# Attention: queries and keys converted in two slots each, both copies of a head's sum ahead of its difference, compressed values split once

## The chip, the cores and the metric

One core of a Trainium2 chip runs the whole kernel. The time is that of one execution on the device in microseconds (us); three executions of the kernel before took 1440.02 to 1446.53 us, with a median of 1442.75 us. Engines are named as in the profile: PE multiplies matrices, DVE (VectorE) and ACT (ScalarE) work elementwise, POOL (GpSimd) does elementwise work and some transfers, SP only issues transfers.

## What is computed

One block of a decoder on 512 tokens of width 2048: a normalised input is projected; a part of it goes through an attention with three branches, another through sliding means, both are merged with gates, projected and added to the input; then a mixture of experts follows. The change concerns the attention. Cut to that:

```python
q, k_slc, k_swa = [_partial_rope(_rms(a, gain), cos, sin) for ...]   # 16 heads, 4 key groups
kc, vc = _compress(k_cmp), _compress(v_cmp)                          # 31 blocks
p_cmp = _masked_softmax(q @ kc * scale, cmp_end <= t); o_cmp = p_cmp @ vc
p     = _masked_softmax(q @ ks * scale, ...);          o_slc = p @ vs
p     = _masked_softmax(q @ kw * scale, ...);          o_swa = p @ vw
o = g0 * o_cmp + g1 * o_slc + g2 * o_swa
attn_branch = einsum("bshd,hde->bshe", o, w_head_out)
```

All is float32. With 512 tokens both the selected and the sliding branch see all earlier tokens.

## The kernel before, in words

Float32 products are made of pairs. A number is stored as a rounded copy and the difference to it; ACT makes the copy, DVE or POOL the difference, and PE multiplies copy by copy, copy by difference and difference by copy, adding up in PSUM (`mm3`, lines 134 to 136; `evac_split`, lines 139 and 140). So almost every product needs an ACT step, then a DVE or POOL step, then PE.

The program is one long list per engine, in the order in which the Python code emits it. `run` (line 201) walks over the pieces of the large projections (`qkv`, `u` for the pooling input, `wp`, `z` for the merge gates, `wo`), and after every part of a piece it makes one `step`: it emits the first function of the list `deferred`, if there is one, and then the functions of the next slot of `side`. The slots of the attention come from a table of numbers, `PLAN` (line 41), by `attention_slots` (line 835). Per group of four heads (four groups, g = 0 to 3) there are in slots relative to the group's start `w0`: the queries `at_q` at -6, the keys `at_k` at -4, the compressed branch `at_c0` to `at_c4` at -4, -2, -1, 1 and 3; and then each head, 8 or 9 slots apart, with four score steps `at_qk`, four scalings `at_scale`, six transposing steps `at_T` (slots 9 to 14), six products `at_pv` (11 to 16) and `at_out` at 18. So the queries and keys of one group lie among the last transposes of the group before.

Names used below. `qn` is the normalised query and key tile; `qT` its transposed queries in PSUM, `q` the pair made of them (partitions 0 to 63 the copy, 64 to 127 the difference); `kT` and `k` (`k1`, `k2`) the same for keys; `kw` the compressed keys. `s` are scores in PSUM, `m` their maxima and sums, `p` the exponentials, `pt` their transpose in PSUM, `pth` and `ptl` the pair made of that, `o` the sum over positions of a head, `oh` and `ol` its pair, `vcg` the compressed values of a group, one block per head, masked by `hmask`. `pl` and `ph` are the pair of the pooling. `qT`, `kT`, `scT` and `s` share one PSUM tile (tag S), and all `pt` share another (tag tr), each with a single buffer: the next transposes wait until both halves of the pair are read out.

After a group's projection, the queries and keys are normalised by steps in `deferred`, one per slot: squares of the first half, squares of the second half, inverse root (12 small instructions), norm, gains, rope. The steps of the pooling share this list.

A head's sum `o` is stored as `oh` (a copy, ACT), `ol` partitions 64 to 127 (the difference, DVE) and `ol` partitions 0 to 63 (a second copy, ACT), in this order (lines 818 to 820); one tile holds both parts of `ol`.

Of the kernel before, what the change touches and what calls it, by code (L numbers as in the profile page):

```python
# [11 lines left out]
F32 = mybir.dt.float32  # L12
# [10 lines left out]
NT = 4  # L23
# [28 lines left out]
    'c0': -4,  # L52
# [24 lines left out]
def hybrid_block_kernel(  # L77
# [37 lines left out]
    def s_tile(name):  # L115
        return psum.tile([128, 2, 512], F32, tag="S", name=name)
# [168 lines left out]
    vcr = mix.tile([128, NKV, 64], F32, name="vcr")  # L285
# [35 lines left out]
    gain = mix.tile([128, 6, 64], F32, name="gain")  # L321
# [18 lines left out]
    def late_loads():  # L340
        q = nc.sync
        for i in range(4):
            q.dma_start(gain[:, i], q_norm_g.to_broadcast([128, 64]))
        q.dma_start(gain[:, 4], k_norm_slc_g.to_broadcast([128, 64]))
        q.dma_start(gain[:, 5], k_norm_swa_g.to_broadcast([128, 64]))
# [187 lines left out]
    def cmp_value():  # L533
# [5 lines left out]
        V.tensor_copy(vcr, po[:, 0:256].rearrange("p (g d) -> p g d", g=4))  # L539
# [50 lines left out]
    def qkv(g):  # L590
# [6 lines left out]
        def done(ps):  # L597
# [13 lines left out]
            q3 = qn.rearrange("p t h d -> p t (h d)")  # L611
# [16 lines left out]
            def gains():  # L628
                V.tensor_tensor(q3, q3, gain.rearrange("p h d -> p (h d)")[:, None, :].to_broadcast([128, NT, 384]),
                                op=OP.mult)  # L630

            def rope():
# [11 lines left out]
            deferred.extend([lambda: squares(0), lambda: squares(1), inverse, norm, gains, rope,  # L644
                             lambda: marks.add(f"qkv{g}")])
# [7 lines left out]
    def at_q(g):  # L653
        att, qn = pools["att"], QN[g]
        st = s_tile(f"qT{g}")
# [4 lines left out]
        for h in range(4):  # L660
            QT[4 * g + h] = att.tile([128, S], F32R, tag="q", name=f"q{g}_{h}", bufs=4)
            A.copy(QT[4 * g + h][0:64], st[64 * (h % 2):64 * (h % 2) + 64, h // 2])
        for h in range(4):
# [3 lines left out]
    def at_k(g):  # L667
# [4 lines left out]
        st = s_tile(f"kT{g}")  # L672
        for t in range(NT):
            T.transpose(st[:, 0, t * 128:(t + 1) * 128], qn[:, t, 4:6].rearrange("p h d -> p (h d)"), ident)
        ur = [(u, slice(64 * r, 64 * r + 64)) for u in range(2) for r in range(2)]
# [62 lines left out]
    def at_c4(g):  # L738
# [3 lines left out]
        for t in range(NT):  # L742
# [5 lines left out]
        vcf = att.tile([128, 4, 64], F32, tag="sm", name=f"vcf{g}")  # L748
        vcg = att.tile([128, 4, 128], F32R, tag="vcg", name=f"vcg{g}")
        V.tensor_tensor(vcf, vcr[:, g, None, :].to_broadcast([128, 4, 64]),  # L750
                        hmask[:, :, None].to_broadcast([128, 4, 64]), op=OP.mult)
        A.copy(vcg[:, :, 0:64], vcf)
        V.tensor_sub(vcg[:, :, 64:128], vcf, f(vcg[:, :, 0:64]))
        pools["vcg", g] = vcg
# [45 lines left out]
    def at_pv(head, i):  # L800
# [13 lines left out]
        if i == 5:  # L814
# [3 lines left out]
            A.copy(oh, o)  # L818
            V.tensor_tensor(ol[64:128], o[0:64], f(oh[0:64]), op=OP.subtract)
            A.copy(ol[0:64], o[0:64])  # L820
# [14 lines left out]
    def attention_slots():  # L835
# [6 lines left out]
        for g in range(NKV):  # L842
# [10 lines left out]
            at(w0 + PLAN['q'], at_q, g)  # L853
            at(w0 + PLAN['k'], at_k, g)
# [742 lines left out]
```

## Time and profile before

| what | value |
|---|---|
| three executions, median | 1442.75 us |
| profiled execution, its time | 1442.58 us |
| profiled execution, its span | 1440.8 us |
| mean granted PE clock | 0.984 |
| PE busy | 1388.4 us, 96% of the span |
| DVE busy | 825.1 us, 57% |
| ACT busy | 765.6 us, 53% |
| POOL busy | 445.4 us, 31% |

The attention runs from about 140 to 800 us, beside the projections. A row of the order of time gives the start in us from the start of the span, the duration, the engine, the line of the kernel, the operation, what it writes and reads, its form and how many were merged; in brackets stands how long the engine had been idle, and what released it. PE is the matrix multiplication, PEld the loading of its weights, which runs beside it.

### The profile page before, as it was taken

The page shows a single profiled execution, that of the slowest core. Times are in us where ns is not written, and L with a number is a line of the kernel's source. Part 1 is how long each engine was busy: PE and PEld are TensorE (multiplying, and loading weights), DVE is VectorE, ACT ScalarE, POOL GpSimd, SP SyncE. Part 2 cuts the span into 40 slices and gives each one's busy share as a digit, 9 for nine tenths or more (in the row PEclk, how much of TensorE's full clock was granted, in tenths as well). Part 3 has the DMA queues.
Part 4 walks back from the last instruction along what each step waited for, and adds up shares of the span by engine and source line. Part 5 has one row for each costly group of instructions (what it writes and reads, how often), then busy time and mean ns, then how long its engine had stood idle before and what let it go on. Part 6 is the DMA issues. An engine that isn't in the chain of part 4 may idle for free.

```text
span 1440.8 us, 18395 instructions
## 1 busy us (share of the span) xinstructions
PE 1388.4 (96%) x6638; PEld 1138.2 (79%) x6638; DVE 825.1 (57%) x1258; ACT 765.6 (53%) x1289; POOL 445.4 (31%) x289
## 2 busy tenths in 40 slices
PE   8998999989999999999999999999999999999995
PEld 7877788778778788788888888888887777777774
DVE  4663773666463453555543202453255899999995
ACT  4543356564666465655665322332242687777784
POOL 0044342322333343243434455211021322222221
PEclk9999999999999999999999999999999999999998
DMA  6344233233333333343434453785675899999994
GB/s 224 94 115 123 80 102 87 77 107 85 91 116 111 92 93 87 96 117 97 109 110 125 117 141 108 224 326 166 226 252 175 279 362 367 367 358 354 330 363 84
DMA packets 193188, 249.88 MB, mean 173 GB/s; under 512 B 50384, under 2 KB 137536, under 8 KB 191264
## 3 DMA queue, kind: packets, MB, share of 16 engines
q1 hardware_dynamic: 176640, 199.13, 43.6%
q0 software_dynamic: 11808, 41.09, 10.0%
q10 hardware_dynamic: 4640, 8.40, 1.6%
q8 instruction: 54, 0.88, 0.3%
q14 instruction: 46, 0.38, 0.1%
HBM read 225.49 MB, written 35.65 MB: 181 GB/s over the span
## 4 chain that ended last, share of the span: by engine, by line
PE 79%; DVE 10%; ACT 6%; issue 2%; DMA 1%; POOL 1%; ACTq 0%; SPq 0%; POOLq 0%; DVEq 0%
PE z L134 7%; PE z L136 7%; PE z L135 7%; PE gu L136 4%; PE gu L134 4%; PE gu L135 4%; PE wo L134 4%; PE wo L136 4%; PE wo L135 4%; PE qkv L135 2%; PE qkv L134 2%; PE qkv L136 2%; PE dn L134 2%; PE dn L135 2%; PE dn L136 2%; PE xT L1245 2%
## 5 line engine op out<-in xcount | busy, mean ns | idle before, releaser
L197 POOL TENSOR_TENSOR lo_z<-raw_z,hi_z 128x1024 fp32r<-128x1024 f32 x64 | 153.4, 2401 | 200.5 <-ACT hi_z L196 192.8
L134 PE MATMUL z<-hT,hi_z 128*128 128x512 f32 x512 | 204.1, 399 | 0.0
L136 PE MATMUL z<-hT,lo_z 128*128 128x512 f32 x512 | 200.7, 392 | 0.0
L135 PE MATMUL z<-hT,hi_z 128*128 128x512 f32 x512 | 200.2, 391 | 0.0
L140 DVE TENSOR_TENSOR ptl<-pt,pth 128x512 fp32r<-128x512 f32 (+1 forms) x96 | 57.8, 602 | 177.0 <-ACT pth L139 176.8
L197 DVE TENSOR_TENSOR lo_gu<-raw_gu,hi_gu 128x2048 fp32r<-128x2048 f32 x64 | 146.8, 2294 | 9.8 <-ACT hi_gu L196 4.2
L196 ACT CAST hi_gu<-raw_gu 128x2048 fp32r<-128x2048 f32 x64 | 122.3, 1911 | 18.7 <-PE gu L136 9.9
L778 ACT ACTIVATE p<-s,m 128x128 f32<-128x128 f32 (+3 forms) x128 | 66.4, 523 | 115.6 <-DVE m L776 112.4
L197 POOL TENSOR_TENSOR lo_qkv<-raw_qkv,hi_qkv 128x1024 fp32r<-128x1024 f32 x28 | 70.6, 2521 | 173.8 <-ACT hi_qkv L196 148.6
L136 PEld LDWEIGHTS z<-hT,lo_z 128*128 128x128 f32 x512 | 96.5, 189 | 21.2
L135 PEld LDWEIGHTS z<-hT,hi_z 128*128 128x128 f32 x512 | 96.7, 189 | 18.6
L134 PEld LDWEIGHTS z<-hT,hi_z 128*128 128x128 f32 x512 | 96.9, 189 | 18.3
L134 PE MATMUL gu<-hi_gu,xh 128*112 128x512 f32 x256 | 106.4, 416 | 0.1
L134 PE MATMUL qkv<-hi_qkv,hT 128*128 128x512 f32 x256 | 103.5, 404 | 0.1
L135 PE MATMUL qkv<-lo_qkv,hT 128*128 128x512 f32 x256 | 101.4, 396 | 0.3 <-POOL lo_qkv L197 0.3
L136 PE MATMUL gu<-hi_gu,xl 128*112 128x512 f32 x256 | 101.7, 397 | 0.0
L136 PE MATMUL qkv<-hi_qkv,hT 128*128 128x512 f32 x256 | 101.5, 396 | 0.0
L134 PE MATMUL wo<-hi_wo,y 128*128 128x512 f32 x256 | 101.1, 395 | 0.0
L135 PE MATMUL gu<-lo_gu,xh 128*112 128x512 f32 x256 | 100.4, 392 | 0.0
L136 PE MATMUL wo<-hi_wo,y 128*128 128x512 f32 x256 | 99.8, 390 | 0.0
L135 PE MATMUL wo<-lo_wo,y 128*128 128x512 f32 x256 | 99.7, 389 | 0.0
L1313 POOL DMA_INDIRECT out_dram<-y,idx x18 | 60.1, 3337 | 107.7 <-ACT hi_gu L196 88.6
(419 smaller groups left out, 3193.7 us busy)
## 6 DMA issues: line engine op xcount, KB each, us to landing
raw_z<-in_w_in_dram SPq DMA_DIRECT2D x128, 256.0 KB
raw_gu<-in_w_expert_gate_dram SPq DMA_DIRECT2D x59, 512.0 KB
raw_gu<-in_w_expert_up_dram SPq DMA_DIRECT2D x59, 512.0 KB
raw_dn<-in_w_expert_down_dram SPq DMA_DIRECT2D x28, 1024.0 KB
raw_wo<-in_w_out_dram SPq DMA_DIRECT2D x32, 512.0 KB
raw_qkv<-in_w_in_dram SPq DMA_DIRECT2D x32, 256.0 KB
raw_qkv<-in_w_in_dram SPq DMA_DIRECT2D x128, 64.0 KB
raw_u<-in_w_in_dram SPq DMA_DIRECT2D x16, 512.0 KB
```

The source lines that it names most:

```text
L134: T.matmul(ps, ah, bh, start=start, stop=False)
L135: T.matmul(ps, ah, bl, start=False, stop=False)
L136: T.matmul(ps, al, bh, start=False, stop=stop)
L140: V.tensor_tensor(lo, src, f(hi), op=OP.subtract)
L196: A.copy(self.hi[sl], self.raw[sl])
L197: self.eng.tensor_sub(self.lo[sl], self.raw[sl], f(self.hi[sl]))
L778: A.activation(p[:, b], v[:, b], AF.Exp, bias=m[:, b:b + 1], scale=0.125, accum_out=m[:, 2 + b:3 + b])
L1245: T.transpose(pt[:, j * RS:(j + 1) * RS], self.xr[:, k0 * 128 + j:(k0 + 4) * 128:4], ident[0:RS, 0:RS])
L1313: ins = G.indirect_dma_start(out=dst, out_offset=bass.IndirectOffsetOnAxis(ap=idx, axis=0), in_=src, in_offset=None, bounds_check=n - 1, o ...
```

## The change

Six edits, which leave PE's rows as they were and in their order:

1. Queries: `at_q` makes the transposes of all four heads and the pairs of two; the pairs of the other two come a slot later (`at_q_half`).
2. Keys: the same in `at_k` and `at_k_half`; `at_c0` comes a slot later, at -3.
3. Head's sum: both ACT copies first, then DVE's difference.
4. Compressed values: they are split into a pair once for all groups (`vhl`, in place of `vcr`), and each group's `vcg` is made by four ACT scalings with `hmask`, in place of a product and a difference on DVE and a copy on ACT.
5. Normalisation: empty steps between the squares, behind them and ahead of the rope, in groups 1 to 3; the gains are held three times in place of six and applied in two instructions (three loads fewer).
6. Pooling: the copy `ph` and the difference `pl` are two steps in place of one.

```diff
-    'c0': -4,
+    'c0': -3,
...
-        V.tensor_copy(vcr, po[:, 0:256].rearrange("p (g d) -> p g d", g=4))
+        pv = po[:, 0:256].rearrange("p (g d) -> p g d", g=4)
+        A.copy(vhl[:, :, 0:64], pv)
+        V.tensor_tensor(vhl[:, :, 64:128], pv, f(vhl[:, :, 0:64]), op=OP.subtract)
...
-                V.tensor_tensor(q3, q3, gain.rearrange("p h d -> p (h d)")[:, None, :].to_broadcast([128, NT, 384]),
+                V.tensor_tensor(qn[:, :, 0:4], qn[:, :, 0:4], gain[:, 0, None, None, :].to_broadcast([128, NT, 4, 64]),
+                                op=OP.mult)
+                V.tensor_tensor(qn[:, :, 4:6], qn[:, :, 4:6], gain[:, None, 1:3].to_broadcast([128, NT, 2, 64]),
                                 op=OP.mult)
...
-            deferred.extend([lambda: squares(0), lambda: squares(1), inverse, norm, gains, rope,
-                             lambda: marks.add(f"qkv{g}")])
+            ready, pause = (lambda: marks.add(f"qkv{g}")), [lambda: None] * (g > 0)
+            deferred.extend([lambda: squares(0), *pause, lambda: squares(1), *pause, inverse, norm, gains, *pause, rope,
+                             ready])
...
-        st = s_tile(f"qT{g}")
+        st = pools["qT"] = s_tile(f"qT{g}")
...
-        for h in range(4):
+        at_q_half(g, 0)
+
+    def at_q_half(g, p):
+        att, st = pools["att"], pools["qT"]
+        for h in (2 * p, 2 * p + 1):
             QT[4 * g + h] = att.tile([128, S], F32R, tag="q", name=f"q{g}_{h}", bufs=4)
             A.copy(QT[4 * g + h][0:64], st[64 * (h % 2):64 * (h % 2) + 64, h // 2])
-        for h in range(4):
+        for h in (2 * p, 2 * p + 1):
...
-        vcf = att.tile([128, 4, 64], F32, tag="sm", name=f"vcf{g}")
-        vcg = att.tile([128, 4, 128], F32R, tag="vcg", name=f"vcg{g}")
-        V.tensor_tensor(vcf, vcr[:, g, None, :].to_broadcast([128, 4, 64]),
-                        hmask[:, :, None].to_broadcast([128, 4, 64]), op=OP.mult)
-        A.copy(vcg[:, :, 0:64], vcf)
-        V.tensor_sub(vcg[:, :, 64:128], vcf, f(vcg[:, :, 0:64]))
-        pools["vcg", g] = vcg
+        vcg = pools["vcg", g] = att.tile([128, 4, 128], F32R, tag="vcg", name=f"vcg{g}")
+        for h in range(4):
+            A.mul(vcg[:, h], f(vhl[:, g]), hmask[:, h:h + 1])
...
             A.copy(oh, o)
+            A.copy(ol[0:64], o[0:64])
             V.tensor_tensor(ol[64:128], o[0:64], f(oh[0:64]), op=OP.subtract)
-            A.copy(ol[0:64], o[0:64])
...
+            at(w0 + PLAN['q'] + 1, at_q_half, g, 1)
             at(w0 + PLAN['k'], at_k, g)
+            at(w0 + PLAN['k'] + 1, at_k_half, g, 1)
...
-            deferred.extend([lambda st=1 << i: double(st) for i in range(g + 1)] + [mean, halves])
+            deferred.extend([lambda st=1 << i: double(st) for i in range(g + 1)] + [mean, half, rest])
```

Where the rows move, at three places. The lines in the rows of the change are those of the changed kernel.

First, the queries of group 1. On ACT before, from the copies of the queries on:

```order
L662 CAST q_0_2716<-qT_2707 64x512
L662 CAST q_1_2718<-qT_2707 64x512
L662 CAST q_2_2720<-qT_2707 64x512
L662 CAST q_3_2722<-qT_2707 64x512
L899 CAST ph_2597<-s_4_2666 128x1024
L830 COPY a_2745<-a_2742 128x512
L831 DMA adram<-a_2745 128x512
L139 CAST pth<-pt_0_2748 128x512
L196 CAST hi_wp_2757<-raw_wp_2755 128x1024
L139 CAST pth<-pt_1_2773 128x512
L677 CAST k_1_2780<-kT_2782 64x512 x4
L699 CAST kw_1244<-kcT 128x32
```

On ACT in the change, from the same copies:

```order
L668 CAST q_0_2716<-qT_2707 64x512
L668 CAST q_1_2718<-qT_2707 64x512
L907 CAST ph_2597<-s_4_2666 128x1024
L836 COPY a_2738<-a_2735 128x512
L837 DMA adram<-a_2738 128x512
L139 CAST pth<-pt_0_2741 128x512
L668 CAST q_2_2748<-qT_2707 64x512
L668 CAST q_3_2750<-qT_2707 64x512
L196 CAST hi_wp_2756<-raw_wp_2754 128x1024
L139 CAST pth<-pt_1_2773 128x512
L687 CAST k_1_2780<-kT_2782 64x512 x2
L139 CAST pth<-pt_2_2808 128x256
```

Two query copies and two key copies now stand behind the next `pth`. On DVE before, from the query differences on:

```order
L665 TENSOR_TENSOR q_0_2716<-qT_2707,q_0_2716 64x512
L665 TENSOR_TENSOR q_1_2718<-qT_2707,q_1_2718 64x512
L665 TENSOR_TENSOR q_2_2720<-qT_2707,q_2_2720 64x512
L665 TENSOR_TENSOR q_3_2722<-qT_2707,q_3_2722 64x512
L900 TENSOR_TENSOR pl_2598<-s_4_2666,ph_2597 128x1024
L140 TENSOR_TENSOR ptl<-pt_0_2748,pth 128x512
L140 TENSOR_TENSOR ptl<-pt_1_2773,pth 128x512
L679 TENSOR_TENSOR k_1_2781<-kT_2782,k_1_2780 64x512 x4
```

On DVE in the change, from the same differences:

```order
L671 TENSOR_TENSOR q_0_2716<-qT_2707,q_0_2716 64x512
L671 TENSOR_TENSOR q_1_2718<-qT_2707,q_1_2718 64x512
L140 TENSOR_TENSOR ptl<-pt_0_2741,pth 128x512
L671 TENSOR_TENSOR q_2_2748<-qT_2707,q_2_2748 64x512
L671 TENSOR_TENSOR q_3_2750<-qT_2707,q_3_2750 64x512
L910 TENSOR_TENSOR pl_2598<-s_4_2666,ph_2597 128x1024
L140 TENSOR_TENSOR ptl<-pt_1_2773,pth 128x512
L689 TENSOR_TENSOR k_1_2781<-kT_2782,k_1_2780 64x512 x2
L140 TENSOR_TENSOR ptl<-pt_2_2808,pth 128x256
L689 TENSOR_TENSOR k_1_2781<-kT_2782,k_1_2780 64x512 x2
```

The first `ptl` moved from behind four differences and `pl` to behind two, and the second pair stands ahead of the second `ptl`.

Second, DVE in the compressed branch of group 1 (`pcl` is the difference of its probabilities). Before:

```order
L140 TENSOR_TENSOR pcl_3079<-pc_3073,pch_3078 128x512
L750 TENSOR_TENSOR vcf_3082<-vcr,hmask 128x256
L753 TENSOR_TENSOR vcg_3083<-vcf_3082,vcg_3083 128x4x64
L783 RECIPROCAL m_1_3042<-m_1_3042 128x2
L900 TENSOR_TENSOR pl_2872<-s_8_3023,ph_2871 128x1024
L772 TENSOR_TENSOR s_2_3115<-s_2_3115,causal 128x2x128
L775 TENSOR_REDUCE m_2_3122<-s_2_3115 128x2
L776 TENSOR_SCALAR m_2_3122<-m_2_3122 128x2
```

In the change:

```order
L140 TENSOR_TENSOR pcl_3079<-pc_3073,pch_3078 128x512
L789 RECIPROCAL m_1_3042<-m_1_3042 128x2
L778 TENSOR_TENSOR s_2_3114<-s_2_3114,causal 128x2x128
L781 TENSOR_REDUCE m_2_3121<-s_2_3114 128x2
L782 TENSOR_SCALAR m_2_3121<-m_2_3121 128x2
L910 TENSOR_TENSOR pl_2872<-s_8_3023,ph_2871 128x1024
```

`vcf` and `vcg` are gone, and `pl` stands behind the next maximum.

Third, DVE in group 2's normalisation, beside the first head of the group's heads that are still running (`sq` and `ss` are the squares and their sums, `pool` a product of the pooling). Before, from the second squares to the inverse's first row:

```order
L920 TENSOR_SCALAR pool_1_3503<-pm_1_3496,cols 128x512
L618 TENSOR_TENSOR sq_1_3506<-qn_3459 128x768
L619 TENSOR_REDUCE ss_3461<-sq_1_3506 128x12
L819 TENSOR_TENSOR ol_3516<-o_3317,oh_3515 64x512
L783 RECIPROCAL m_3_3423<-m_3_3423 128x2
L772 TENSOR_TENSOR s_0_3525<-s_0_3525,causal 128x256
L775 TENSOR_REDUCE m_0_3530<-s_0_3525 128x2
L776 TENSOR_SCALAR m_0_3530<-m_0_3530 128x2
L920 TENSOR_SCALAR pool_3_3552<-pm_3_3545,cols 128x512
L622 TENSOR_SCALAR ss_3461<-ss_3461 128x24
```

In the change, from the head's difference `ol`:

```order
L826 TENSOR_TENSOR ol_3513<-o_3317,oh_3512 64x512
L789 RECIPROCAL m_3_3423<-m_3_3423 128x2
L778 TENSOR_TENSOR s_0_3522<-s_0_3522,causal 128x256
L781 TENSOR_REDUCE m_0_3527<-s_0_3522 128x2
L782 TENSOR_SCALAR m_0_3527<-m_0_3527 128x2
L930 TENSOR_SCALAR pool_3_3549<-pm_3_3542,cols 128x512
L617 TENSOR_TENSOR sq_1_3552<-qn_3459 128x768
L618 TENSOR_REDUCE ss_3461<-sq_1_3552 128x12
L140 TENSOR_TENSOR ptl<-pt_0_3555,pth 128x512
L789 RECIPROCAL m_0_3527<-m_0_3527 128x2
L140 TENSOR_TENSOR ptl<-pt_1_3594,pth 128x512
```

The second squares moved from ahead of `ol` to behind the head's maximum, and the inverse, whose twelve rows stood ahead of the head's first `ptl`, now begins four rows below the last one shown, ahead of the third `ptl`.

## Rows read from the trace of the kernel before

**Rows 1.** The page, part 2: PE's busy tenths in 40 equal slices.
```profile
PE   8998999989999999999999999999999999999995
```

**Rows 2.** A stretch: us, busy us of each engine (instructions), PEclk, DMA share, GB/s.
```profile
100.00:800.00 700.00, 671.97 (x3239) 558.59 (x3238) 357.85 (x682) 385.35 (x870) 252.10 (x122) 0.99 0.37 101
```

**Rows 3.** Order of time, group 1: start, us, instruction, count, [idle before <- releaser].
```profile
319.60 2.80 DVE L665 TENSOR_TENSOR q<-qT,q 64x512 fp32r<-64x512 f32 x4 [4.03 <-ACT q L662]
...
321.52 0.59 ACT L139 CAST pth<-pt 128x512 fp32r<-128x512 f32 x1 [0.40 <-ACT a L830]
...
324.43 1.11 PE L797 MATMUL pt<-ident,p 128*128 128x128 f32 x4 [3.96 <-DVE ptl L140]
...
325.34 1.06 PE L674 MATMUL kT<-ident,qn 128*128 128x128 f32 x4
```

**Rows 4.** Order of time, the same place in group 2.
```profile
484.08 0.59 ACT L139 CAST pth<-pt 128x512 fp32r<-128x512 f32 x1 [0.40 <-ACT a L830]
...
485.73 1.12 PE L797 MATMUL pt<-ident,p 128*128 128x128 f32 x4 [3.34 <-DVE ptl L140]
...
486.64 1.06 PE L674 MATMUL kT<-ident,qn 128*128 128x128 f32 x4
```

**Rows 5.** Order of time, groups 1 and 2, from c4 to the scores.
```profile
361.83 0.41 ACT L752 CAST vcg<-vcf 128x256 fp32r<-128x256 f32 x1 [2.31 <-DVE vcf L750]
...
369.19 0.50 PE L769 MATMUL s<-k,q 128*128 128x512 f32 x1 [2.57 <-ACT p L778]
...
526.35 0.50 PE L769 MATMUL s<-k,q 128*128 128x512 f32 x1 [0.58 <-ACT p L778]
```

**Rows 6.** Order of time, group 2's first head with the norm steps.
```profile
412.01 0.58 ACT L820 CAST ol<-o 64x512 fp32r<-64x512 f32 x1 [2.18 <-DVE ol L819]
...
413.63 0.33 PE L797 MATMUL pt<-ident,p 128*128 128x128 f32 x1 [2.15 <-ACT p L787]
...
413.74 0.17 DVE L622 TENSOR_SCALAR ss<-ss 128x24 f32<-128x24 f32 x1
...
416.13 0.18 DVE L131 SCALAR_TENSOR_TENSOR ss<-rtmp,ss 128x24 f32<-128x24 f32 x1
...
423.13 1.75 DVE L629 TENSOR_TENSOR qn<-qn,gain 128x1536 f32<-128x1536 f32 x1
...
425.27 0.42 PEld L797 LDWEIGHTS pt<-ident,p 128*128 128x128 f32 x4 [0.21 <-DVE ptl L140]
```

**Rows 7.** Stretches behind three gaps, columns as in rows 2.
```profile
163.60:167.00 3.40, 3.40 (x11) 2.62 (x10) 0.81 (x2) 3.18 (x5) 0.00 (x0) 0.50 0.02 5
324.00:327.50 3.50, 3.07 (x12) 2.79 (x13) 1.07 (x2) 1.64 (x3) 1.86 (x1) 0.51 0.11 18
484.50:491.30 6.80, 5.57 (x17) 4.75 (x18) 3.00 (x5) 4.23 (x8) 1.00 (x1) 0.50 0.40 117
```

**Rows 8.** Groups by form: count, busy us, mean ns | idle before, releaser.
```profile
L819 DVE TENSOR_TENSOR ol<-o,oh 64x512 fp32r<-64x512 f32 x16 | 10.9, 684 | 24.8 <-ACT oh L818 24.6
...
L787 ACT ACTIVATE p<-p,m 128x128 f32<-128x128 f32 x32 | 10.9, 387 | 0.0
...
L820 ACT CAST ol<-o 64x512 fp32r<-64x512 f32 x16 | 9.3, 581 | 17.2 <-DVE ol L819 17.2
```

**Rows 9.** Order of time, group 0: the query and key chain, then a head.
```profile
162.65 1.09 PE L658 MATMUL qT<-ident,qn 128*128 128x128 f32 x8 [2.28 <-DVE qn L642]
...
177.42 0.50 PE L709 MATMUL scT<-q,kw 128*128 128x512 f32 x1 [0.33 <-DVE kw L700]
...
177.47 1.22 DVE L895 SCALAR_TENSOR_TENSOR s<-s,u 128x1024 f32<-128x1024 f32 x1
...
220.54 0.66 PE L797 MATMUL pt<-ident,p 128*128 128x128 f32 x4 [0.58 <-DVE ptl L140]
```

**Rows 10.** Order of time, group 0: POOL's difference beside DVE's gains.
```profile
155.92 3.20 POOL L197 TENSOR_TENSOR lo_u<-raw_u,hi_u 128x1024 fp32r<-128x1024 f32 x1 [3.04 <-ACT hi_u L196]
...
156.91 3.83 DVE L629 TENSOR_TENSOR qn<-qn,gain 128x1536 f32<-128x1536 f32 x1
```

More of the change, by code (lines that the diff above doesn't have):

```diff
@@ L284, in hybrid_block_kernel @@
     gates = mix.tile([128, NT, 48], F32, name="gates")
-    vcr = mix.tile([128, NKV, 64], F32, name="vcr")
+    vhl = mix.tile([128, NKV, 128], F32R, name="vhl")
     kcT = mix.tile([128, 128], F32, name="kcT")
@@ L320, in hybrid_block_kernel @@
     sc = mix.tile([128, 5, 2, 8], F32, name="sincos")
-    gain = mix.tile([128, 6, 64], F32, name="gain")
+    gain = mix.tile([128, 3, 64], F32, name="gain")
     posi = early.tile([128, 5], I32, name="posi")
@@ L341, in late_loads @@
         q = nc.sync
[L342 to L345, printed above, removed]
+        for i, g_ in enumerate((q_norm_g, k_norm_slc_g, k_norm_swa_g)):
+            q.dma_start(gain[:, i], g_.to_broadcast([128, 64]))
         q.dma_start(gainc, k_norm_cmp_g.to_broadcast([128, 64]))
@@ L610, in done @@
             q2 = qn.rearrange("p t h d -> p (t h) d")
-            q3 = qn.rearrange("p t h d -> p t (h d)")
             rs = ss[:, 1].rearrange("p t h -> p (t h)")
@@ L671, in at_k, with at_k_half @@
         KK[g] = (k1, k2)
-        st = s_tile(f"kT{g}")
+        st = pools["kT"] = s_tile(f"kT{g}")
         for t in range(NT):
             T.transpose(st[:, 0, t * 128:(t + 1) * 128], qn[:, t, 4:6].rearrange("p h d -> p (h d)"), ident)
-        ur = [(u, slice(64 * r, 64 * r + 64)) for u in range(2) for r in range(2)]
+        at_k_half(g, 0)
+    def at_k_half(g, u):
+        (k1, k2), st = KK[g], pools["kT"]
+        ur = [(u, slice(64 * r, 64 * r + 64)) for r in range(2)]
         for u, rr in ur:
@@ L896, in mean, with half, rest @@
                 V.tensor_tensor(s[:, :, 0:w - 1], e[:, :, 0:w - 1], u[:, :, 0:w - 1], op=OP.subtract)
-            def halves():
+            def half():
                 A.copy(ph, cur[0])
+            def rest():
                 V.tensor_sub(pl, cur[0], f(ph))
```

## The prediction

> **What bounds the kernel now.** I read the page first, then the stretches, then TensorE's (PE's) idle time with its releasers, last the order of time around each gap. PE's row of slices is at nine tenths or more from the attention's end almost to the last slice [rows 1]. A stage with PE full cannot get shorter here, since PE's own instructions and their order are the same before and after. What can be won lies where PE stands idle: in the stretch from 100 to 800 us, which holds the whole attention, PE is busy 671.97 of 700 us [rows 2]. So 28 us is the ceiling, less what belongs to the end of the projection. These idle spells are single gaps, and each has a cause in VectorE (DVE) or ScalarE (ACT) queues a few us earlier. The largest are: 3.96 us in group 1 and 3.34 us in group 2, where the transposes `pt` wait for the difference `ptl` behind the query work [rows 3, 4]; 2.57 us in group 1, where the scores `s` wait for an exponential [rows 5]; 2.15 us in group 2, where `pt` waits for a scaled `p` [rows 6]. After the gaps of rows 3 and 4 the granted clock is 0.51 for 3.5 us and 0.50 for 6.8 us, the lower of its two levels, 1.2 GHz [rows 7].
>
> **The change, part by part.**
>
> *Compressed values (c4).* DVE loses `vcf` and the `vcg` difference in each group, and ACT loses one copy and its wait for `vcf`, 2.31 us in group 1 [rows 5]. ACT gains four scalings of 128x128; the same form takes 387 ns [rows 8], so 4 x 0.39 = 1.5 us at most, less than the 2.31 us wait they replace plus the copy of 0.41. Behind them on ACT are the reciprocal's product, the scaled `p` and the next exponentials. In group 1 the pooling difference `pl` also moves behind the next maximum on DVE. Since ACT and DVE both lose over 2 us ahead of the exponential on which PE waited 2.57 us, I count that gap as gone, and likewise the 0.58 us of group 2 [rows 5]: **-3.15**. Should ACT's four be twice as dear, 1.5 us more would still leave half of the gap closed. The one-time split of `vhl` runs before the first attention work, with DVE idle behind it: 0.
>
> *Queries in two slots.* Before, DVE stands idle for 4.03 us until ACT has made its copies, four differences then take 2.80 us from 319.60, and `ptl` stands behind them and `pl` [rows 3]. Now ACT makes two copies of 0.58 [rows 8], 1.2 us less ahead of `pth`, and DVE two differences, and then `ptl`. In group 1 the head's sum comes earlier too, with its two ACT copies side by side, so DVE's difference and what follows it start up to 0.58 later; so `pth` moves from 321.52 to about 320.9, `ptl` ends at 322.2 and `pt` starts at 322.3 in place of 324.43. But the key transposes `kT` come next on PE, and `kT` takes the PSUM tile of `qT`; it must wait for the second pair: two more ACT copies behind `pth` (2 x 0.58, to 322.7) and two differences (1.4, to 324.1). `kT` then starts at 324.15 in place of 325.34: **-1.2**. In group 2 nothing delays DVE: `pth` at 484.08 - 1.18 = 482.9, `pt` at 484.25, the second pair done at 486.1, `kT` at 486.1 in place of 486.64 [rows 4]: **-0.5**. So one long gap becomes two, the second behind the second pair. Groups 0 and 3 had no such gap.
>
> *The clock behind these gaps.* At half rate 3.5 and 6.8 us cost 1.7 and 3.4 us [rows 7]. The gaps left, about 1.8 + 1.25 us in each group, are 0.2 to 0.9 us shorter in sum than before; the 2.57 us of rows 5 was followed by no stretch at the low level, the 2.28 us gap ahead of `qT` in group 0 was, at half rate in the trace just behind it [rows 7, 9]. Bounds 0 and 5.1; I take one stretch of the three: **-1.7**.
>
> *Heads' sums.* ACT's second copy no longer waits for DVE's difference (17.2 us over 16 heads [rows 8]), but the difference now waits for that copy. Where DVE came late, as in group 2 behind the squares, this helps: ACT stood idle for 2.18 us until 412.01, so oh was done at 409.8; ACT's copy now ends at 410.4 and the difference at 411.1 in place of 412.0, and the scaling of `p` stands behind the difference and not behind ACT's copy, another 0.3 less: `p` is ready about 1.15 us sooner, and the gap of 2.15 shrinks to 1.0 [rows 6]. That is given back: the twelve small steps of the inverse (413.74 to 416.3, 2.6 us) move from in front of the head's first `ptl` to in front of its third, where the gains (1.75) stood; the weight load behind that `ptl` already waits 0.21 [rows 6], so PE waits 2.6 - 1.75 = 0.9 more. Together **-0.25**. Where DVE was waiting for oh, 24.8 us idle in all [rows 8], the scaling of `p` now starts after ACT's copy, the difference and the reciprocal (0.58 + 0.68 + 0.2 behind oh) in place of the difference and the copy (0.68 + 0.58), 0.2 later. Between no cost, where PE comes later than `p`, and 16 x 0.2 = 3.2 I take **+0.9**, nearer the low end, because only some heads have `pt` at the heels of `p`.
>
> *`pl` a step later.* In group 0 `ptl` is no longer behind `pl`, and the 0.58 us gap there goes [rows 9]: **-0.55**.
>
> *Keys in two slots, `c0` a slot later.* The second pair of key differences and `kw` come behind a step of other work. In group 0 this is the pooling's mean, 1.22 us and two small steps; `scT` already waits 0.33 for `kw` [rows 9]. I take 0.8 there and 0.2 in each later group, between 0 and 1.5 each: **+1.4**.
>
> *Gains in two instructions, norm steps further apart.* The same 1536 elements with one start more: **+0.1** in group 0, where `qT` waits for this chain. The pauses fill slots of later heads; the rope still ends well ahead of `qT`. Three loads fewer on SP's queue: they land long before use, 0.
>
> Here one row speaks of more. The gains of group 0 took 3.83 us where those of group 2 took 1.75, while POOL's `lo_u` ran from 155.92 for 3.20 us [rows 6, 10]. So DVE work that lands beside a POOL difference can lose some 2.1 us. The Trainium skill, "SBUF — State Buffer", section "Who interferes with whom", says that a DVE instruction with two SBUF inputs and a GpSimd instruction that reads SBUF exclude each other for a whole instruction, and that ACT waits for neither; the rows agree. By it the move of `vcg` to ACT is safe, and each moved norm step is a new ticket: one loss of 2.1 us in front of a waiting `pt` would take the sum to 1439.6.
>
> The sum: -3.15 - 1.2 - 0.5 - 1.7 - 0.25 - 0.55 + 0.9 + 1.4 + 0.1 = -4.95. The profiled execution took 1442.58 us, 0.2 below the median of the three runs (1442.75), so I forecast **1437.5 us**, -0.35%. The runs shown spread from 1440.02 to 1446.53, so about 0.5% (7.2 us) is what can be told from no change; my forecast lies inside that.
>
> **The rivals.**
>
> *Faster: the clock stays up and the small costs hide.* If the shorter pairs of gaps leave the clock at its upper level in both groups (3.4 more) and PE never meets `p` or `kw` late (2.3 more), it comes to 1431.8. For it: the gap of 2.57 us without a drop. Against it: both pairs still sum to about 3 us with some 0.6 us of work between, and the 2.28 us gap was followed by a drop.
>
> *Slower: the norm steps in front of `ptl`.* Squares, inverse, norm, gains and rope of groups 1 to 3 now stand in more slots, each in front of some `ptl` or `ol`. Where DVE is the late engine, PE pays the difference. If in each of the three groups the inverse costs 0.9 as in group 2, one step loses 2.1 to POOL, and the query and clock gains fail as well (3.4 us), it comes to 1437.5 + 2 x 0.9 + 3 x 2.1 + 3.4 = 1449, +0.45%; it ends above today's time once these steps cost over 1.7 us in each group. Against it: DVE has only 358 busy us of 700 here [rows 2], and outside the places named the `ptl` wait for ACT, not for DVE.
>
> *The halves do not do what they say.* If DVE's first pair still starts only when ACT is through with all four, or `kT` waits so long for the second pair that nothing is won, the query terms and the clock go (3.4): 1440.9. For it: before, the first difference did wait for all four copies although it needs one.
>
> **How the numbers follow.** My forecast, with its terms within about 3 us, 0.57; the halves without effect 0.11; faster 0.25; slower 0.07. Of the forecast, some 0.02 lies beyond 0.5% faster. So faster 0.27, same 0.66, slower 0.07. The range from 1431.5 to 1443.5 takes the clock term's far end with most of the fast case, and no gain at all on the other side; it leaves out the slow case and the lower half of the fast one.
>
> **What would show it.** The profile after should show: no `vcf`, four ACT scalings per group without a wait, and no gap at `s` at the places of rows 5; two DVE query differences starting after ACT's second copy, a gap at `pt` of about 1.8 us in groups 1 and 2 and a new one of about 1.2 at `kT`; a gap of about 0.9 at the fourth `pt` of the head behind the inverse in group 2; ACT's second copy of a head's sum without idle time, and DVE's difference 0.6 later. PE should stay full after 800 us. It is wrong if the sum of PE's gaps from 100 to 800 falls by much more or less than 3 us besides the clock, if new gaps at `pt` or `o` exceed those removed, or if the low clock after `qT` lasts as long as before.

## The result and the profile after

The changed kernel is slower: a median of 1453.52 us in five runs (1450.47 to 1455.84), against 1445.04 us for five runs of the kernel before (1440.02 to 1446.53); the ratio is 1.0074, 95% interval 1.006 to 1.0088. The forecast was 1437.5 us. The profiled execution has a span of 1454.1 us, 13.3 more than before. It is the slowest of the five, 2.3 us above their median, and at 0.980 its mean granted clock is the lowest (0.982 to 0.985 in the others), so its span overstates the change. These are the page's first line, PE's line of its part 1 and PE's row of slices, after the change.

```profile
span 1454.1 us, 18414 instructions
...
PE 1396.6 (96%) x6638; PEld 1142.7 (79%) x6638; DVE 826.1 (57%) x1254; ACT 768.4 (53%) x1302; POOL 443.0 (30%) x289
...
PE   9998899989999999989999999999999999999996
```

PE has the same 6638 instructions, so I put its 8.2 us more of busy time (1388.4 before) down to the clock; the other 5.1 us are idle time. Stretches of the changed kernel show where (us, busy us of PE, PEld, DVE, ACT and POOL with counts, PEclk, DMA share, GB/s); the first holds what [rows 2] held, work that now lasts some 12 us longer.

```profile
100.00:812.00 712.00, 677.29 (x3237) 560.71 (x3236) 358.53 (x677) 388.24 (x883) 251.34 (x122) 0.98 0.36 99
```
```profile
327.70:331.10 3.40, 3.40 (x10) 2.68 (x9) 3.37 (x3) 1.16 (x2) 1.42 (x1) 0.50 0.21 52
488.20:495.00 6.80, 6.08 (x17) 4.93 (x18) 2.72 (x4) 2.43 (x4) 2.37 (x1) 0.50 0.30 77
641.80:645.20 3.40, 3.40 (x11) 2.63 (x10) 0.65 (x1) 3.00 (x6) 0.00 (x0) 0.51 0.61 196
665.60:669.00 3.40, 3.40 (x10) 2.63 (x9) 0.00 (x0) 0.59 (x1) 0.00 (x0) 0.50 0.61 154
1116.20:1126.40 10.20, 9.53 (x31) 7.87 (x31) 5.77 (x36) 1.01 (x3) 0.00 (x0) 0.50 0.73 245
1133.30:1136.70 3.40, 3.22 (x12) 2.62 (x13) 1.25 (x2) 1.06 (x2) 1.34 (x2) 0.51 0.19 58
```

In the attention PE now idles 712 - 677.29 = 34.7 us in place of 28.0. The stretches at 1.2 GHz behind the old places of [rows 7] are as long as before, there are two new ones at 641.8 and 665.6, and at the start of the experts there are 13.6 us at half rate in two stretches, where before there was this one.

```profile
1105.80:1112.50 6.70, 6.70 (x20) 5.64 (x21) 4.32 (x27) 0.21 (x1) 0.00 (x0) 0.50 0.83 304
```

So 6.7 us of the loss are idle time in the attention, and the longer time at half rate costs 6.8 us more: 3.4 in the attention and 3.4 at the experts. The second half of that need not belong to the change: over 1100 to 1140 us PE's granted clock is 0.91 before and 0.83 here, and 0.91 again in the two runs further down that take one difference off POOL and keep the rest of the change.

Now the places that the prediction named, in the order of time after the change (start us, us, instruction, count, [idle before <- releaser]).

```profile
322.15 1.39 DVE L671 TENSOR_TENSOR q<-qT,q 64x512 fp32r<-64x512 f32 x2 [2.84 <-ACT q L668]
...
325.44 0.33 PE L803 MATMUL pt<-ident,p 128*128 128x128 f32 x1 [1.85 <-DVE ptl L140]
...
327.21 0.33 PE L680 MATMUL kT<-ident,qn 128*128 128x128 f32 x1 [1.11 <-DVE q L671]
...
364.41 1.29 ACT L760 ACTIVATE vcg<-vhl,hmask 128x128 fp32r<-128x128 f32 x4
...
371.09 0.39 PE L775 MATMUL s<-k,q 128*128 128x512 f32 x1
...
414.18 0.33 PE L803 MATMUL pt<-ident,p 128*128 128x128 f32 x1 [0.91 <-ACT p L793]
...
427.68 0.33 PE L803 MATMUL pt<-ident,p 128*128 128x128 f32 x1 [0.88 <-DVE ptl L140]
...
487.15 0.33 PE L803 MATMUL pt<-ident,p 128*128 128x128 f32 x1 [1.85 <-DVE ptl L140]
488.92 0.48 PE L680 MATMUL kT<-ident,qn 128*128 128x128 f32 x1 [1.11 <-DVE q L671]
```

The long gap of [rows 3, 4] has become two, 1.85 at `pt` and 1.11 at `kT`, in groups 1 and 2; the scores of [rows 5] wait for nothing; the 2.15 of [rows 6] is 0.91, with a new 0.88 behind the inverse. All these numbers were forecast. The loss stands at places where no gap was:

```profile
317.00 2.24 DVE L904 TENSOR_TENSOR s<-pe,u 128x14 f32<-128x14 f32 x1
...
315.81 3.40 POOL L197 TENSOR_TENSOR lo_u<-raw_u,hi_u 128x1024 fp32r<-128x1024 f32 x1 [3.54 <-ACT hi_u L196]
...
320.50 0.33 PE L803 MATMUL pt<-ident,p 128*128 128x128 f32 x1 [1.67 <-ACT p L793]
...
336.44 2.20 DVE L710 TENSOR_TENSOR kw<-kcT,kw 128x32 fp32r<-128x32 f32 x1
...
336.25 2.35 POOL L197 TENSOR_TENSOR lo_qkv<-raw_qkv,hi_qkv 128x1024 fp32r<-128x1024 f32 x1 [7.12 <-ACT hi_qkv L196]
...
338.70 0.51 PE L719 MATMUL scT<-q,kw 128*128 128x512 f32 x1 [1.68 <-DVE kw L710]
...
635.45 1.45 DVE L639 TENSOR_TENSOR rt<-qn,sincos 128x192 f32<-128x192 f32 x1
...
637.48 2.66 DVE L642 TENSOR_TENSOR qn<-rt 128x192 f32<-128x192 f32 x1
...
640.44 0.68 DVE L826 TENSOR_TENSOR ol<-o,oh 64x512 fp32r<-64x512 f32 x1
...
635.35 1.34 POOL L960 TENSOR_TENSOR th<-ld 128x512 f32<-128x512 f32 x1 [3.86 <-DVE ld L959]
...
637.56 2.36 POOL L197 TENSOR_TENSOR lo_z<-raw_z,hi_z 128x1024 fp32r<-128x1024 f32 x1
...
641.18 0.50 PE L833 MATMUL a<-oh,woh 128*128 128x512 f32 x1 [3.94 <-DVE ol L826]
...
662.75 2.21 DVE L710 TENSOR_TENSOR kw<-kcT,kw 128x32 fp32r<-128x32 f32 x1
...
665.01 0.50 PE L719 MATMUL scT<-q,kw 128*128 128x512 f32 x1 [1.68 <-DVE kw L710]
```

The pattern is always the same. A small DVE step that reads SBUF only, which takes 0.2 to 0.4 us elsewhere, starts within 0.2 us of a POOL difference or addition, or while one runs, and ends at most 0.25 us behind it; then something that PE waits for follows on DVE or ACT. A `kw` difference of 128x32 took 2.20 us so. The rope of group 3, which ended at 618.3 us before, now stands directly in front of the head's difference `ol`, and two of its six steps took 4.11 us in place of 0.7. In group 3 `kw` meets a `lo_z` that starts at 662.57 and costs another 1.68. In group 0 the second pair of key differences and `kw` stand behind the pooling's mean, whose first step of 128x2 took 1.84 us beside `lo_wp` (0.15 before):

```profile
174.46 1.84 DVE L901 TENSOR_TENSOR pe<-s,icnt 128x2 f32<-128x2 f32 x1
...
173.88 2.39 POOL L197 TENSOR_TENSOR lo_wp<-raw_wp,hi_wp 128x1024 fp32r<-128x1024 f32 x1 [5.22 <-ACT hi_wp L196]
...
179.33 0.47 PE L718 MATMUL scT<-q,kw 128*128 128x512 f32 x1 [2.33 <-DVE k L689]
```

### The profile page after: what moved, and what is told of

The parts are those of the page before. It is cut to its first block, busy times and chain, and to the rows that moved or that the text cites. A ratio compares the mean times of both kernels' runs of the same rounds, so it can differ in the third digit from the quotient of the medians.

```text
span 1454.1 us, 18414 instructions
## 1 busy us (share of the span) xinstructions
PE 1396.6 (96%) x6638; PEld 1142.7 (79%) x6638; DVE 826.1 (57%) x1254; ACT 768.4 (53%) x1302; POOL 443.0 (30%) x289
## 4 chain that ended last, share of the span: by engine, by line
PE 81%; DVE 9%; ACT 6%; issue 2%; DMA 1%; POOL 0%; ACTq 0%; SPq 0%; POOLq 0%; DVEq 0%
PE z L134 7%; PE z L136 7%; PE z L135 7%; PE gu L136 4%; PE gu L134 4%; PE gu L135 4%; PE wo L134 4%; PE wo L136 4%; PE wo L135 4%; PE qkv L134 3%; PE qkv L135 3%; PE qkv L136 3%; PE o L818 2%; PE dn L134 2%; PE xT L1255 2%; PE dn L135 2%
```

## The experiments

Two theories. **A, collisions:** the lost time is that of DVE steps that start beside a POOL difference. **B, order:** the moved steps are late because of what now stands ahead of them, whatever POOL does. Ratios are against the kernel before, run on the same chip, with 95% intervals.

**The rope a slot earlier.** Only the last of the three empty steps is taken out.

```diff
-            deferred.extend([lambda: squares(0), *pause, lambda: squares(1), *pause, inverse, norm, gains, *pause, rope,
+            deferred.extend([lambda: squares(0), *pause, lambda: squares(1), *pause, inverse, norm, gains, rope,
```

> The changed kernel without the empty step ahead of the rope, so in groups 1 to 3 the rope is emitted a slot earlier and no longer stands in front of the head's difference ol at 635 us. Theory A (collisions: DVE steps that read SBUF only lose up to 2.4 us when they start beside a POOL difference, and stand in front of something PE waits for): the gap of 3.94 us at the head's output and the half-clock stretch behind it go, 3.9 + 1.7 = 5.6 us, so about 1448, unless the rope meets another POOL difference where PE waits for it (then up to 1451). Theory B (order: the later places of many DVE steps cost by themselves, a little at each, whatever POOL does): the rope's own six steps are 2.1 us, so not more than 2 us come back, 1451.5 or more.

Measured: ratio 1.0046 (1.0029 to 1.0062). The rope's six steps take 0.34 to 0.36 us each at 631.3, and neither the gap nor the half-clock stretch at the head's output is there. By the ratio that is 4.0 us of the 5.6 expected, within an uncertainty of about 3. The placement alone does not tell A from B, since the rope has left `ol` as well.

**No empty steps.**

```diff
-            ready, pause = (lambda: marks.add(f"qkv{g}")), [lambda: None] * (g > 0)
+            ready, pause = (lambda: marks.add(f"qkv{g}")), []
```

> The changed kernel with none of the empty steps: the norm chain of groups 1 to 3 stands in consecutive slots, as before the change. Theory A: as without the rope's pause, about 1448 (5.6 us less than the change), and no more, because the other pauses are behind no gap of their own. Theory B: the pauses of squares and inverse cost as well, so some 2 us less than with the rope's pause alone removed.

Measured: 1.0050 (1.0033 to 1.0066), no better than the rope's alone, so the further 2 us that B expected did not come. The gap at `ol` is gone, but in group 1 the second of the two gain instructions took 2.88 us beside `lo_wp`, and `pt` waited 2.40 us for a scaled `p` where it waited 0.12 in the change. One collision was traded for another. And the head of [rows 6] waits 1.88 us at `pt`, where it waited 0.91 in the change, and nothing behind the inverse: these two numbers belong to the empty steps.

**Keys and c0 as before.**

```diff
-    'c0': -3,
+    'c0': -4,
...
-        ur = [(u, slice(64 * r, 64 * r + 64)) for r in range(2)]
+        ur = [(u, slice(64 * r, 64 * r + 64)) for u in range(2) for r in range(2)]
...
-            at(w0 + PLAN['k'] + 1, at_k_half, g, 1)
```

> The changed kernel with keys in one slot and the compressed keys c0 at -4 again, all else as changed. Both theories expect the waits of scT for kw and k to go: 1.9 us in group 0, 2.1 in group 1, 3.5 with the clock in group 3, 0.4 in group 2, together 8 us, so about 1445.5. Theory A adds that the time of the kw difference falls from 2.20 to 0.2 us only where it no longer starts beside a POOL difference. If the keys do not matter, 1453.

Measured: 1.0028 (1.0018 to 1.0037), so 0.0046 of the 0.0074 is this edit, some 6.6 us, a little under the 8 expected. `scT` waits 0.32 us in group 0 and nothing worth telling elsewhere; the longest `kw` difference is 0.85 us. The gap at `ol` stays (3.92).

**The compressed keys split once.** DVE's `kw` difference goes from each group; the order of the rest stays.

```diff
-        V.tensor_copy(kcT, pt[:, 0:128])
+        A.copy(kch, pt[:, 0:128])
+        V.tensor_tensor(kcl, pt[:, 0:128], f(kch), op=OP.subtract)
...
-        A.copy(kw1[:, 96:128], kcg)
-        V.tensor_sub(kw2[:, 96:128], kcg, f(kw1[:, 96:128]))
+        A.copy(kw1[:, 96:128], f(kch[:, 32 * g:32 * g + 32]))
+        A.copy(kw2[:, 96:128], f(kcl[:, 32 * g:32 * g + 32]))
```

> The changed kernel with the compressed keys split once for all groups, as the compressed values are, so each group's kw is two ACT copies of 128x32 and no DVE difference; the order of everything else stays (kw1 and kw2 share a tile with common zeros). Theory A (collision): the waits of 1.68 us at scT in groups 1 and 3 fall below 0.4 us and the half-clock stretch behind the second goes; in group 0 the wait stays near 2, because there the key differences stand behind the pooling mean. Together about 5 us, 1448.5. Theory B (order): scT waits for the key differences of the second slot anyway; the gaps stay above 1 us, 1452 or more.

Measured: 1.0062 (1.0046 to 1.0079); span 1449.3 us. The trace does what A said: in groups 1 and 3 `scT` runs behind the key differences without the 1.68 us (nothing, and 0.23 for the keys), and in group 0 the wait is still 2.35. The span is 4.8 us shorter than that of the change; the ratio shows only 1.7 us, and its interval overlaps that of the change. The stretch at 665.6 is gone, but the one behind the 3.86 us left at `ol` is 6.8 us long (clock 0.51) in place of 3.4. The rows are the first that B cannot have: the key differences are where they were.

**One POOL difference on DVE.** The one beside `kw` in group 1 is given to DVE, where it stands behind `kw`.

```diff
-    'lo': {'qkv': 'VGVGVGVGGGGGGGGGGGGGGGGGGGGGGGGG', 'u': 'G', 'wp': 'GGGGVGVV', 'z': 'G', 'w': 'GGV', 'cmp':
+    'lo': {'qkv': 'VGVGVGVGGGGGGGGGVGGGGGGGGGGGGGGG', 'u': 'G', 'wp': 'GGGGVGVV', 'z': 'G', 'w': 'GGV', 'cmp':
```

> The changed kernel with one of POOL's differences (lo_qkv, the one that starts at 336.25 us, just ahead of the kw difference of group 1) on DVE, where it is emitted behind the kw difference; all that stands ahead of kw in DVE's queue is as in the change. Theory A (collision): kw takes 0.19 us in place of 2.20 at the same place in its queue, and the wait of 1.68 us at scT in group 1 goes (below 0.2); the same wait in group 3 stays at 1.68. Theory B (order): kw is as late as before, and both waits stay.

Two rows of this run: DVE in group 1, and all `kw` differences (ns least, median, most, first and last start).

```profile
340.72 0.20 DVE L710 TENSOR_TENSOR kw<-kcT,kw 128x32 fp32r<-128x32 f32 x1
```
```profile
L710 DVE TENSOR_TENSOR kw<-kcT,kw x4: 193/194/2209, 180.9 to 663.5; 128x32 fp32r<-128x32 f32 x4
```

The same instruction behind the same instructions takes 0.20 us when POOL is quiet, and the wait at `scT` is gone; in group 3, where nothing was changed, it still takes 2.21 and PE waits 1.68. This settles A for `kw`: its wait of 1.68 us in group 1 is in all four traces that have the step beside `lo_qkv` (the change, the rope a slot earlier, no empty steps, and the next run). The run is one execution (1452.69 us, where the kernel before has a median of 1442.57), read by its rows.

**The same at the rope.** The `lo_z` beside the rope of group 3 is given to DVE, behind `ol`; the rope stays where the change put it.

```diff
-    'lo': {'qkv': 'VGVGVGVGGGGGGGGGGGGGGGGGGGGGGGGG', 'u': 'G', 'wp': 'GGGGVGVV', 'z': 'G', 'w': 'GGV', 'cmp':
+    'lo': {'qkv': 'VGVGVGVGGGGGGGGGGGGGGGGGGGGGGGGG', 'u': 'G', 'wp': 'GGGGVGVV', 'z': 'GGGGGGGGGGGGGGGGGGGGGGVGGGGGGGGGGGGGGGGGGGGGGGGGGGGGGGGGGGGGGGGG', 'w': 'GGV', 'cmp':
```

> The changed kernel with one of POOL's differences (lo_z, the one that starts at 637.56 us beside the rope of group 3) on DVE, where it is emitted behind the head's difference ol; the rope stays in front of ol. Theory A (collision): the rope's step of 2.66 us takes 0.36, 2.3 us less, and the gap of 3.94 us at the head's output falls to about 1.6 (the rope's six steps of 0.35 and the 1.1 us that the second loses beside POOL's addition for the merge stay in front). Theory B (order: it is the rope's place in front of ol): the gap stays above 3.5. Behind ol the reciprocal now waits 1.2 us longer, which may show at the next pt.

DVE and PE at that place in this run:

```profile
634.54 1.45 DVE L639 TENSOR_TENSOR rt<-qn,sincos 128x192 f32<-128x192 f32 x1
...
636.56 0.36 DVE L642 TENSOR_TENSOR qn<-rt 128x192 f32<-128x192 f32 x1
...
637.22 0.69 DVE L826 TENSOR_TENSOR ol<-o,oh 64x512 fp32r<-64x512 f32 x1
637.94 1.23 DVE L197 TENSOR_TENSOR lo_z<-raw_z,hi_z 128x1024 fp32r<-128x1024 f32 x1
...
637.96 0.50 PE L833 MATMUL a<-oh,woh 128*128 128x512 f32 x1 [1.60 <-DVE ol L826]
...
640.42 0.47 PE L803 MATMUL pt<-ident,p 128*128 128x128 f32 x1 [1.40 <-ACT p L793]
```

2.66 has become 0.36 and 3.94 has become 1.60, as A had it. So of the largest gap 2.3 us are one collision, and the 1.60 left holds the rope's place and 1.1 us of the other (1.45, beside POOL's addition for the merge). The difference itself now stands in front of the reciprocal, and `pt` waits 1.40 for it; the time of this one execution was 1451.75 us. The clock did not follow the gap: the stretch at half rate at this place is 6.8 us long (639.2 to 646.0, 0.50, with the wait of 1.40 in it) in place of 3.4. And in this run and the one before it the clock stays at 1.00 over the 3.4 us behind the wait of 1.68 at `scT` in group 3, where the change had 0.50. So these runs give no fixed price in clock for a gap. The other collisions (group 0, `kw` in group 3, the pooling's step in group 1) are read by the same pattern, without a run of this kind.

**The edits left.** No empty steps, and keys as before: what remains are queries, sums, values, gains and pooling.

```diff
-            ready, pause = (lambda: marks.add(f"qkv{g}")), [lambda: None] * (g > 0)
+            ready, pause = (lambda: marks.add(f"qkv{g}")), []
...
-            at(w0 + PLAN['k'] + 1, at_k_half, g, 1)
```

> The changed kernel without the empty steps and with keys and c0 as before; what is left are the queries in two slots, the heads' sums, the compressed values, the split gains and the pooling in two steps. Theory A: the two losses add up, about 5 (pauses) + 7 (keys) below the change, which is about 4 us below the kernel before, ratio 0.997. If the left edits lose as well (the queries' and the heads' sums' part), ratio 1.000 or more.

Measured: 0.9988 (0.9978 to 0.9998), between the two answers. So pauses and keys together carry all of the slowdown: 0.0086, which these intervals don't tell from the 0.0070 of the two alone. What is left is worth 1.7 us, not 4.

**Each of these alone, on the kernel before.** Queries:

```diff
-        for h in range(4):
+        at_q_half(g, 0)
...
+            at(w0 + PLAN['q'] + 1, at_q_half, g, 1)
```

> The kernel before with the queries in two slots and nothing else. The prediction's terms: the gap at pt of 3.96 us in group 1 becomes 1.8 at pt and 1.2 at kT, that of 3.34 in group 2 becomes 1.8 and 0.9, in sum -1.7, and -1.7 for the clock: ratio 0.998. Rival: the gap ahead of pt from a scaled p (1.67 us in the change, where the pooling's small difference took 2.24 us beside a POOL difference) comes with this edit: then group 1 gains nothing, ratio 1.000.

Measured: 0.9997 (0.9987 to 1.0006). `pt` and `kT` wait 1.36 and 0.99 in group 1 and 2.15 and 1.11 in group 2, so 1.6 us less in group 1 and 0.1 in group 2, where 1.2 and 0.5 were forecast: the sum of 1.7 is right by two misses that cancel. The gap of 1.67 does not come with this edit. The clock gives nothing back in sum: group 2's stretch is 3.4 us in place of 6.8, and a new one of 3.4 (0.52) stands behind the 2.56 us at `s`, which had none before. Heads' sums:

```diff
             A.copy(oh, o)
+            A.copy(ol[0:64], o[0:64])
             V.tensor_tensor(ol[64:128], o[0:64], f(oh[0:64]), op=OP.subtract)
-            A.copy(ol[0:64], o[0:64])
```

> The kernel before with both ACT copies of a head's sum ahead of DVE's difference, and nothing else. The prediction's terms: the gap of 2.15 us in group 2 falls to about 1.0, the inverse is moved in front of the third ptl (+0.9), and elsewhere +0.9 in all: +0.65 us, ratio 1.0005. Rival: the later scaling shows at one place as a gap of 1.7 us at pt in group 1 (the head's sum stands 0.6 us later there and the pooling's small steps meet a POOL difference): +2 us, ratio 1.0015.

Measured: 1.0018 (1.0004 to 1.0033): the rival, whose 1.0015 the ratio doesn't tell from 1.0005, but whose gap is there. The pooling's last step before, then DVE and PE in group 1 of this run, and the head of [rows 6]:

```profile
315.32 0.17 DVE L896 TENSOR_TENSOR s<-pe,u 128x14 f32<-128x14 f32 x1
```
```profile
315.29 2.24 DVE L897 TENSOR_TENSOR s<-pe,u 128x14 f32<-128x14 f32 x1
...
318.79 0.33 PE L798 MATMUL pt<-ident,p 128*128 128x128 f32 x1 [1.68 <-ACT p L788]
...
415.76 0.33 PE L798 MATMUL pt<-ident,p 128*128 128x128 f32 x1 [1.85 <-ACT p L788]
```

DVE's difference now starts 0.5 us later behind `oh`, since it waits for the second ACT copy; and that copy no longer waits for DVE, so ACT's next work, `hi_u`, and with it POOL's `lo_u` come 0.9 us earlier (`lo_u` starts 1.0 us behind the difference, 2.3 before). Both push the pooling's three steps behind the difference into a `lo_u` which they had just escaped: before, the last of them ended at 315.5, when `lo_u` started. The prediction's own term did not come with this edit: the 2.15 of [rows 6] falls to 1.85 and not to 1.0, and there is no 0.9 behind the inverse. Values and pooling:

```diff
+            A.mul(vcg[:, h], f(vhl[:, g]), hmask[:, h:h + 1])
...
-            deferred.extend([lambda st=1 << i: double(st) for i in range(g + 1)] + [mean, halves])
+            deferred.extend([lambda st=1 << i: double(st) for i in range(g + 1)] + [mean, half, rest])
```

> The kernel before with the compressed values split once, the gains in two instructions (without which the tiles don't fit) and the pooling's pair in two steps, and nothing else. The prediction's terms: the gaps at s of 2.57 and 0.58 us go, the gap of 0.58 in group 0 goes, +0.1 for the gains: -3.6 us, ratio 0.9975. Rival: the gap at s was followed by none at the next pt only because PE came late; the work behind it moves up and another wait takes 1 to 2 us of it back, ratio 0.999.

Measured: 0.9951 (0.9935 to 0.9968), 1435.7 us against 1442.16: faster than both kernels, and the lowest ratio of this study (the split of the values is that of the change, and the gains are in two). It is twice the gain forecast, and in part luck. The three gaps are gone as forecast, and 1.26 of [rows 3] with them, and idle time is 3.8 us less in all; the other 2.3 us of span are PE's busy time, 1386.1 us, as the long gaps of groups 1 and 2 have no stretch at half rate behind them here. One gap came new, with a stretch of 3.4 us (0.51) behind it:

```profile
277.66 2.89 DVE L630 TENSOR_TENSOR qn<-qn,gain 128x512 f32<-128x512 f32 x1
...
277.39 2.62 POOL L197 TENSOR_TENSOR lo_wp<-raw_wp,hi_wp 128x1024 fp32r<-128x1024 f32 x1 [7.11 <-ACT hi_wp L196]
...
282.93 0.47 PE L795 MATMUL pt<-ident,p 128*128 128x128 f32 x1 [2.65 <-ACT p L785]
```

"One start more" in the gains was a second step in front of `ol`, and it met `lo_wp`. So the next run takes the gains in one instruction again; room for its larger tile comes from common zeros of `kw1` and `kw2` and a shared tag.

```diff
+                V.tensor_tensor(q3, q3, gain.rearrange("p h d -> p (h d)")[:, None, :].to_broadcast([128, NT, 384]),
...
+        pools["kw1"], pools["kw2"] = kw[:, 0:224], kw[:, 128:352]
```

> The kernel before with the compressed values split once and the pooling's pair in two steps, but the gains in one instruction again (room comes from kw1 and kw2 sharing a tile with common zeros, and the pooling's small tile sharing the tag of another). With the gains in two, the second one took 2.89 us in place of 0.68 beside a POOL difference, and pt waited 2.65 us at 282.9. Theory A: that gap falls to the 0.4 us of the kernel before, 2.2 us less: ratio 0.9935. Rival: with gains in one, the rope's first step meets the same POOL difference (as in the kernel before, 1.64 in place of 0.35), and another wait takes more than half of it back: 0.995.

Measured: 0.996 (0.9948 to 0.9973), which leaves A's ratio out and the rival's in, and overlaps that of the run before. The gap fell from 2.65 to 0.30 us as A said. As the rival said, the rope's first step took 1.64 us beside `lo_wp`; of what came back, a wait for the pooling at `pm` that grew from 0.23 to 1.20 us is the largest part. The span is 1437.4 us against 1434.7, because PE's busy time is 3.5 us longer. Group 2 shows how. Behind the same gap of 3.3 us at `pt`, the first run (`pt` at 482.25) kept its clock and the second (at 481.02) did not:

```profile
482.00:489.00 7.00, 6.75 (x35) 5.67 (x36) 4.00 (x7) 4.34 (x8) 1.97 (x2) 1.00 0.30 76
```
```profile
481.00:488.00 7.00, 6.98 (x24) 5.90 (x25) 3.25 (x5) 4.07 (x7) 1.36 (x1) 0.61 0.29 76
```

Last, queries on top of that (the query lines as above).

> The same with the queries in two slots as well. By the gaps of the run with the queries alone (-1.6 us in group 1, -0.1 in group 2) about 1.5 us less than without them: ratio 0.9925; if the compressed values have already taken a part of that gap in group 1 (2.70 us there in place of 3.96), nothing: 0.9935.

Measured: 0.9982 (0.9968 to 0.9996), worse than without and outside both answers. The gaps of group 1 are 1.17 and 1.11, but the shift brought `pl` beside `lo_wp` (3.04 us in place of 1.22) and `kw` beside `lo_qkv` (1.94), and `pt` waited 1.61 us for the `ptl` behind them. That cancels the gain: PE's idle time is 47.5 us, 47.8 without the queries. The 2.2 us by which the span is longer than without the queries are PE's busy time (1392.1 against 1389.6), so clock, and no run shows why.

## Why the prediction was wrong

The sum of -4.95 failed at three terms: the keys, put at +1.4, cost 5.6 us of idle time; the empty steps, put at 0, put the rope in front of `ol`, which cost 3.9; and the clock, put at -1.7, lost 3.4 us in the attention. Behind the first two lies one step of the working: a moved DVE step was priced by what stands ahead of it in its queue, and it can take as long as the POOL instruction beside it.

- **Compressed values (-3.15) and `pl` (-0.55):** right. The gaps went. Alone, with the gains in two, these edits gave 0.0049, 7 us, of which the gaps are about half.
- **Queries (-1.2, -0.5):** right in mechanism, nearly in size: 3.96 became 1.85 + 1.11, 3.34 became the same, -1.0 and -0.4. Alone they gave -1.6 and -0.1, and no time clear of noise.
- **Clock (-1.7):** wrong in sign. Both stretches stayed and two were added, 3.4 us at half rate each (1.7 us lost); with the longer time at the experts PE's busy time rose by 8.2 us. The new ones stand behind new gaps, but other runs have the same gap without a stretch, or a longer stretch behind a shorter gap. What decides it is open, and so is the cause of the 3.4 us at the experts.
- **Heads' sums (-0.25, +0.9):** in group 2 the numbers are right to 0.1 us (0.91 for 1.0, 0.88 for 0.9), but under the wrong edit. With the sums alone the 2.15 became 1.85 and the 0.88 did not come; with everything but the empty steps it was 1.88. The term counted on a free DVE, and it is the empty step between the squares that clears it. The +0.9 was a drift spread over 16 heads; what came was one collision of 1.67.
- **Keys and c0 (+1.4):** "0.8 there and 0.2 in each later group, between 0 and 1.5 each" failed. It was 2.0 in group 0 and 1.7 in groups 1 and 3, above the bound, and 0.3 more at the keys of group 3. In group 0 about 1.7 of it is, by my estimate, the pooling's step of 1.84 us in place of 0.15; in groups 1 and 3 it is `kw` itself. I had bounded the wait by what stands ahead on DVE, and not by what `kw` itself can take.
- **Norm steps further apart (0):** "the rope still ends well ahead of `qT`" is true and the wrong question. `qT` reads the rope; `ol` merely stands behind it in DVE's queue, and that cost 3.94 us, 2.3 of it one collision, and 1.7 of clock in this execution. The prediction's own slow rival had this mechanism, squares to rope "in front of some `ptl` or `ol`" and a loss of 2.1 to POOL, at 1449 us; it was given 0.07, with DVE's half-empty queue as the reason. A half-empty queue is no protection where a step can take as long as POOL's.
- **Gains in two (+0.1):** no cost to be seen in the change; 2.4 to 2.65 us at `pt` in the three runs where the second met `lo_wp` (those without the empty steps but with the gains in two).

The rule that the prediction cited from the Trainium skill ("SBUF — State Buffer", section "Who interferes with whom") holds here: 0.20 us without POOL's difference and 2.20 beside it, the same step in the same place. I had weighed it as one further loss of 2.1 us, when nearly every edit of this change moves steps of that kind. [rows 2] would have given an estimate: POOL is busy 252 of 700 us, so a step put at an arbitrary time starts beside POOL work in about a third of the cases.

## What to carry to other kernels

When a change moves small VectorE steps that read SBUF only, price each by the length of the GpSimd instruction it may meet times GpSimd's busy share (an estimate that no run here tested), and ask what stands behind it in its queue, not only who reads it. Edits that take such a step off VectorE altogether (the compressed values, the compressed keys) could be forecast here gap by gap, though not the clock behind the gaps; edits that only shift them in time deal the collisions anew, and a gain of 1 to 2 us each is of the size of one collision. Test such edits one by one: here the good one, worth 0.4 to 0.5 per cent with its share of clock, was buried under two others; and a term that comes out right in the whole change can still belong to another edit.

## What was not expected of the hardware

The loss is not in proportion to the step's size: 128x2, 128x14 and 128x32 elements took 1.84, 2.24 and 2.20 us, each to the end of the POOL difference beside it. It goes both ways: the `lo_u` at 315.81, beside the pooling's 128x1024 step, took 3.40 us in place of 2.40. And it isn't for two-input steps alone: the scaling of the maxima, one tensor of 128x2 by a constant, took 2.14 us beside a `lo_u`. The same section of the Trainium skill counts scalings by a constant among the steps that can take both ports, and this row agrees.

```profile
310.16 2.14 DVE L782 TENSOR_SCALAR m<-m 128x2 f32<-128x2 f32 x1
...
309.88 2.40 POOL L197 TENSOR_TENSOR lo_u<-raw_u,hi_u 128x1024 fp32r<-128x1024 f32 x1 [5.73 <-ACT hi_u L196]
```

A difference with one input in PSUM lost nothing: this `ptl` started inside a `lo_z` that runs from 621.75 us for 2.40.

```profile
622.18 0.69 DVE L140 TENSOR_TENSOR ptl<-pt,pth 128x512 fp32r<-128x512 f32 x1 [1.11 <-ACT pth L139]
```

The mean granted clock is not the same in every execution of one kernel: the last kernel above took 1435.14 us at 0.988 and 1442.95 us at 0.984.
